# Longer instructions in the body and a halved row at the end of a ReLU row-sum on one Trainium2 core

## The chip, the cores and the metric

The kernel runs on one core of a Trainium2 chip. The metric is the device time of one execution in microseconds (us), without the host. The profile of an execution covers a *span* that begins with the kernel's first DMA issue and ends with its last wait. The time is longer than the span, by 1.35 us in the kernel before (called *time outside the span* below). A result lists the time and the span of every run; spans are listed to 0.1 us.

Engine names in the profile: DVE is VectorE, ACT is ScalarE, SPq is the sequencer that issues the DMAs. A *semaphore* is a counter: in the kernel's code one engine or a DMA raises it (`then_inc`), and another engine waits until it has reached a value (`wait_ge`).

## The reference

```python
x = np.random.randn(32, 512, 1024).astype(np.float32)
out = np.sum(np.maximum(x, 0), axis=-1)          # (32, 512) float32
```

64 MiB are read and 64 KiB are written.

## The kernel before

The 16,384 rows lie on 128 partitions, 128 rows per partition. Seven chunks of 16 rows per partition (8 MiB each) come first. Then comes the tail: transfers of 8, 4, 2 and 1 rows (the one-row transfer is *row 14*), then the last row in three parts of 576, 256 and 192 columns. Three chunk buffers rotate. The tail reuses the buffer of chunk 4, so it can be issued only when VectorE has finished that chunk.

```python
STEPS = [4, 5, 7]; MIXED = [3, 4, 5]
TAIL = [8, 4, 2, 1]; LAST = [576, 256, 192]
# issue on the SP queue: chunk c waits until VectorE has done chunk c - 3
for c in range(NBIG + 1):
    if c >= NB:
        sp.wait_ge(s_dve, 3 * (c - NB + 1))
    if c < NBIG:
        sp.dma_start(out=buf[:, c % NB, :, :], in_=...).then_inc(s_in[c], 16)
# ... the tail's transfers, then (later) the two stores

# chunks 0 to 5: ScalarE does the ReLU in place, VectorE sums the rows
for i, n in enumerate(steps):
    t = buf[:, b, r : r + n, :]
    act.activation(t, t, AF.Relu).then_inc(s_act, 1)
    dve.wait_ge(s_act, 3 * c + i + 1)
    dve.tensor_reduce(out=res[...], in_=t, axis=X, op=ALU.add).then_inc(s_dve, 1)
# ... chunk 6 and the tail: whole rows, ReLU and sum in one instruction, alternating engines

# the last row
act.wait_ge(s_in[-3], 16)
on_act(parts[0], last[:, n : n + 1]).then_inc(s_tact, 1)
dve.wait_ge(s_in[-2], 16)
on_dve(parts[1], last[:, n + 1 : n + 2]).then_inc(s_tpart, 1)
dve.wait_ge(s_tpart, 1)
dve.wait_ge(s_in[-1], 16)
dve.wait_ge(s_tact, 1)
on_dve(last[:, :], res[:, J - 1 : J]).then_inc(s_tdve, 1)   # third part plus the two partial sums
```

## Time and profile before

| | before |
|---|---|
| time, median of 3 runs | 161.24 us (161.21 to 161.25) |
| span of the profiled run (161.23 us) | 159.88 us |
| time outside the span, that run | 1.35 us |
| VectorE busy / ScalarE busy | 122.0 / 101.0 us |
| input DMA | 434 GB/s while it streams |

These are lines of the profile page: the span, each engine's busy time (share of the span, number of instructions), the DMA queues (packets, MB, share of the 16 engines' time), and the chain of waits by line.

```profile
span 159.9 us, 148 instructions
...
DVE 122.0 (76%) x58; ACT 101.0 (63%) x55; POOL 0.2 (0%) x4
...
q1 hardware_dynamic: 2304, 67.18, 97.9%
q14 instruction: 1, 0.01, 0.0%
...
DMA buf<-in_x_dram 69%; ACT buf L129 18%; DVE res L131 10%; DVE buf L112 1%; SPq L89 1%; DVE last L112 0%; DVEq L163 0%
```

The data queue (q1) occupies the DMA engines for 97.9% of the span. Queue q14, which the page lists as instruction, carried one packet of 8 KiB (0.01 MB on the page); it comes up again below.

Next is the table by stages of the kernel before. Each line is a stretch between the arrivals of two chunks: its bounds, its length, busy time and count for VectorE, ScalarE and GpSimd, then granted clock, DMA share and GB/s.

```profile
core 0: us, DVE busy (x) ACT busy (x) POOL busy (x), PEclk, DMA share, GB/s
21.84:41.19 19.35, 15.12 (x3) 14.04 (x4) 0.00 (x0) 1.00 1.00 434
...
99.23:118.59 19.36, 17.48 (x4) 14.04 (x4) 0.00 (x0) 1.00 1.00 433
118.59:137.94 19.35, 17.59 (x9) 12.71 (x8) 0.00 (x0) 1.00 0.94 406
```

An 8 MiB chunk arrives every 19.35 us, at 434 GB/s, and no engine needs that long for it (VectorE at most 17.59 us, ScalarE 14.04), so the body is bound by input DMA. (The 0.94 in the last stretch does not mean a gap: the arrivals keep their period.)

Finally, the timeline of the kernel before: start, duration, engine, source line, operation, operands, count, and in brackets the idle time before and what ended it.

```profile
21.84 14.04 ACT L129 ACTIVATE buf<-buf 128x4096 f32<-128x4096 f32 x3 [19.77 <-DMA buf<-in_x_dram]
25.48 9.85 DVE L131 TENSOR_REDUCE res<-buf 128x4 f32<-128x4096 f32 x2 [25.48 <-ACT buf L129]
...
120.95 1.82 SPq L89 DMA_DIRECT2D buf<-in_x_dram  x4
...
156.32 1.22 DVE L112 TENSOR_SCALAR_CACHE_REDUCE buf<-buf 128x1024 f32<-128x1024 f32 x1
157.08 0.68 ACT L109 ACTIVATE buf<-buf 128x576 f32<-128x576 f32 x1 [0.90 <-DMA buf<-in_x_dram]
157.47 0.08 DVE L112 DVE_READ_ACCUMULATOR buf<-buf 128x1 f32 x1
157.47 0.41 DVE L112 TENSOR_SCALAR_CACHE_REDUCE buf<-buf 128x256 f32<-128x256 f32 x1
...
158.02 0.36 DVE L112 TENSOR_SCALAR_CACHE_REDUCE last<-last 128x194 f32<-128x194 f32 x1
...
158.41 0.34 SPq L168 DMA_DIRECT2D out_dram<-res  x1
```

Row 14 lands at 156.30. VectorE then works through row 14, the 256 columns, three waits and the last part one after the other. The last 192 columns landed at 157.68 (the DMA completions in the trace), yet the last instruction starts only at 158.02: at the end VectorE, not DMA, holds the kernel for about 0.34 us.

### The profile page before, as it was taken

Reading aid. Unit: us, or ns where it says so; the run is one execution under the profiler, and the core shown is the slowest. Engines: PE = TensorE matmul, PEld = TensorE weight load, DVE = VectorE, ACT = ScalarE, POOL = GpSimd, SP = SyncE. Lnnn points to the kernel's source line nnn. Section 1 sums busy time; section 2 is a strip of 40 time slices with the busy share of each in tenths; the row PEclk is TensorE's granted clock in tenths of the full one; section 3 lists DMA queues with packets and bytes.
Section 4 is the critical chain, followed back from the end, with each engine's and each line's share of the span. In section 5 each row is a group of like instructions: output and inputs, shape, how many; then the busy total and the mean of one; then the engine's idle time right before and its main releaser. Section 6 shows DMA issues by size and latency. Waiting matters only on the chain.

```text
span 159.9 us, 148 instructions
## 1 busy us (share of the span) xinstructions
DVE 122.0 (76%) x58; ACT 101.0 (63%) x55; POOL 0.2 (0%) x4
## 2 busy tenths in 40 slices
DVE  0000006989879897998969989699899999598995
ACT  3000059990699808996099941999339980496972
POOL 0000000000000000000000000000000000000000
DMA  7996996996996997989979969969969969899993
GB/s 262 525 525 262 525 525 262 525 525 262 525 492 295 525 459 328 525 377 410 525 312 476 525 262 525 525 262 525 525 262 525 525 262 525 385 402 394 414 407 116
DMA packets 2305, 67.18 MB, mean 420 GB/s; under 512 B 512, under 2 KB 768, under 8 KB 1024
## 3 DMA queue, kind: packets, MB, share of 16 engines
q1 hardware_dynamic: 2304, 67.18, 97.9%
q14 instruction: 1, 0.01, 0.0%
HBM read 67.11 MB, written 0.07 MB: 420 GB/s over the span
## 4 chain that ended last, share of the span: by engine, by line
DMA 69%; ACT 18%; DVE 11%; SPq 1%; issue 0%; DVEq 0%
DMA buf<-in_x_dram 69%; ACT buf L129 18%; DVE res L131 10%; DVE buf L112 1%; SPq L89 1%; DVE last L112 0%; DVEq L163 0%
## 5 line engine op out<-in xcount | busy, mean ns | idle before, releaser
L131 DVE TENSOR_REDUCE res<-buf 128x4 f32<-128x4096 f32 (+3 forms) x18 | 100.4, 5604 | 33.6 <-ACT buf L129 33.6
L129 ACT ACTIVATE buf<-buf 128x4096 f32<-128x4096 f32 (+3 forms) x18 | 80.8, 4553 | 46.3 <-DMA buf<-in_x_dram 46.3
L109 ACT ACTIVATE buf<-buf 128x1024 f32<-128x1024 f32 (+1 forms) x18 | 18.4, 1024 | 9.8 <-DMA buf<-in_x_dram 9.8
L112 DVE TENSOR_SCALAR_CACHE_REDUCE buf<-buf 128x1024 f32<-128x1024 f32 (+1 forms) x19 | 21.3, 1173 | 2.7 <-DMA buf<-in_x_dram 2.5
L109 ACT ACTIVATION_READ_ACCUMULATOR buf<-buf 128x1 f32 x18 | 3.4, 186 | 0.0
L129 ACT ACT_TABLE_LOAD x1 | 1.3, 1283 | 0.8 <-PEq L184 0.8
L112 DVE DVE_READ_ACCUMULATOR buf<-buf 128x1 f32 x19 | 1.6, 83 | 0.0
L112 DVE TENSOR_SCALAR_CACHE_REDUCE last<-last 128x194 f32<-128x194 f32 x1 | 0.4, 356 | 0.1
L184 POOL MEMSET const-bfloat16-1.0<- 128x1 bf16 x1 | 0.1, 102 | 0.0
L184 POOL MEMSET const-uint8-127<- 128x1 uint8 x1 | 0.1, 102 | 0.0
L184 POOL MEMSET const-float32-0.0<- 128x1 f32 x1 | 0.1, 100 | 0.2 <-issue 0.2
L184 POOL MEMSET const-float32-1.0<- 128x1 f32 x1 | 0.1, 99 | 0.0
L112 DVE DVE_READ_ACCUMULATOR last<-last 128x1 f32 x1 | 0.1, 83 | 0.0
## 6 DMA issues: line engine op xcount, KB each, us to landing
buf<-in_x_dram SPq DMA_DIRECT2D x1, 4096.0 KB, 26.7
buf<-in_x_dram SPq DMA_DIRECT2D x1, 2048.0 KB, 31.2
buf<-in_x_dram SPq DMA_DIRECT2D x1, 1024.0 KB, 33.2
buf<-in_x_dram SPq DMA_DIRECT2D x1, 512.0 KB, 34.0
buf<-in_x_dram SPq DMA_DIRECT2D x1, 288.0 KB, 34.3
buf<-in_x_dram SPq DMA_DIRECT2D x1, 128.0 KB, 34.1
buf<-in_x_dram SPq DMA_DIRECT2D x7, 36.3
last<-in_x_dram SPq DMA_DIRECT2D x1, 96.0 KB, 33.9
```

The lines of the kernel that those rows point to most:

```text
L89: sp.dma_start(out=buf[:, tb, r : r + n, :], in_=xv[-1][:, r : r + n, :]).then_inc(s_in[NBIG + i], 16)
L109: return act.activation(t, t, AF.Relu, accum_out=acc)
L112: return dve.tensor_scalar(out=t, in0=t, scalar1=0.0, scalar2=None, op0=ALU.max, op1=ALU.add, accum_out=acc)
L129: act.activation(t, t, AF.Relu).then_inc(s_act, 1)
L131: dve.tensor_reduce(out=res[:, c * BIG + r : c * BIG + r + n], in_=t, axis=X, op=ALU.add).then_inc(s_dve, 1)
L184: nc = _bacc.Bacc("TRN2", target_bir_lowering=False, num_devices=1)
```

## The change

The intent has two parts. In the body, fewer instructions with less fixed cost (estimated from the groups by form of the kernel before, about 0.15 us for each reduce on VectorE and 0.2 us for each activation on ScalarE): chunk 0 in one step of 16 rows, chunks 1 to 3 in steps of 7 and 9. At the end, a shorter serial chain on VectorE: row 14 is split between the two engines, and the last row is cut 512, 256, 256. The diff, cut to its core:

```diff
-STEPS = [4, 5, 7]
-MIXED = [3, 4, 5]
+STEPS = [[16], [7, 9], [7, 9], [7, 9], [4, 5, 7], [3, 4, 5]]
-LAST = [576, 256, 192]
+LAST = [512, 256, 256]
+    half = nc.alloc_sbuf_tensor("half", [P, 2], fp32)
...
-            sp.wait_ge(s_dve, 3 * (c - NB + 1))
+            sp.wait_ge(s_dve, done[c - NB])
...
+    r, _, s = tail[-1]
+    act.wait_ge(s, 16)
+    dve.wait_ge(s, 16)
+    on_act(buf[:, tb, r, 0 : D // 2], half[:, 0:1]).then_inc(s_half, 1)
+    on_dve(buf[:, tb, r, D // 2 : D], half[:, 1:2]).then_inc(s_half, 1)
+    dve.wait_ge(s_half, 2)
+    dve.tensor_tensor(
+        out=res[:, j0 + r : j0 + r + 1], in0=half[:, 0:1], in1=half[:, 1:2], op=ALU.add
+    )
...
-    dve.wait_ge(s_tpart, 1)
+    dve.wait_ge(s_part, 2)
     dve.wait_ge(s_in[-1], 16)
-    dve.wait_ge(s_tact, 1)
```

More of the change, by code (lines that the diff above doesn't have):

```diff
@@ L6 @@
 BIG = 16
-NTWO = 6
 NB = 3
@@ L57, in bass_relu_sum_kernel @@
     s_fdve = nc.alloc_semaphore("s_fdve")
-    s_tact = nc.alloc_semaphore("s_tact")
-    s_tpart = nc.alloc_semaphore("s_tpart")
+    s_half = nc.alloc_semaphore("s_half")
+    s_part = nc.alloc_semaphore("s_part")
     s_tdve = nc.alloc_semaphore("s_tdve")
@@ L64, in bass_relu_sum_kernel @@
     sp, act, dve = nc.sync, nc.scalar, nc.vector
+    NTWO = len(STEPS)
+    done = [sum(map(len, STEPS[: c + 1])) for c in range(NTWO)]
     tb = NBIG % NB
@@ L117, in row @@
         return buf[:, c % NB, i, :], res[:, c * BIG + i : c * BIG + i + 1]
-    for c in range(NTWO):
-        b, steps = c % NB, STEPS if c < NTWO - 1 else MIXED
+    k = 0
+    for c, steps in enumerate(STEPS):
         act.wait_ge(s_in[c], 16)
-        if steps is MIXED:
+        alone = BIG - sum(steps)
+        if alone:
             dve.wait_ge(s_in[c], 16)
-            for i in (BIG - 4, BIG - 3):
+            for i in range(BIG - alone, BIG - alone // 2):
                 on_dve(*row(c, i))
         r = 0
-        for i, n in enumerate(steps):
-            t = buf[:, b, r : r + n, :]
+        for n in steps:
+            t = buf[:, c % NB, r : r + n, :]
             act.activation(t, t, AF.Relu).then_inc(s_act, 1)
-            dve.wait_ge(s_act, 3 * c + i + 1)
+            k += 1
+            dve.wait_ge(s_act, k)
             dve.tensor_reduce(
@@ L134, in bass_relu_sum_kernel @@
             r += n
-        if steps is MIXED:
-            for i in (BIG - 2, BIG - 1):
-                on_act(*row(c, i))
+        for i in range(BIG - alone // 2, BIG):
+            on_act(*row(c, i))
     j0 = NBIG * BIG
@@ L147, in bass_relu_sum_kernel @@
                 ins.then_inc(s_fact if i % 2 else s_fdve, 1)
-    for r, n, s in tail:
-        if n > 1:
-            act.wait_ge(s, 16)
+    for r, n, s in tail[:-1]:
+        act.wait_ge(s, 16)
         dve.wait_ge(s, 16)
@@ L154, in bass_relu_sum_kernel @@
             f(buf[:, tb, i, :], res[:, j0 + i : j0 + i + 1])
+    r, _, s = tail[-1]
+    act.wait_ge(s, 16)
+    dve.wait_ge(s, 16)
[5 more added lines that the diff above has]
+    )
     n = LAST[2]
     act.wait_ge(s_in[-3], 16)
-    on_act(parts[0], last[:, n : n + 1]).then_inc(s_tact, 1)
+    on_act(parts[0], last[:, n : n + 1]).then_inc(s_part, 1)
     dve.wait_ge(s_in[-2], 16)
-    on_dve(parts[1], last[:, n + 1 : n + 2]).then_inc(s_tpart, 1)
-    dve.wait_ge(s_tpart, 1)
+    on_dve(parts[1], last[:, n + 1 : n + 2]).then_inc(s_part, 1)
+    dve.wait_ge(s_part, 2)
     dve.wait_ge(s_in[-1], 16)
-    dve.wait_ge(s_tact, 1)
     on_dve(last[:, :], res[:, J - 1 : J]).then_inc(s_tdve, 1)
```

## The prediction

> **What bounds the kernel now.** Input DMA, from end to end. The table by stages shows 434 GB/s and DMA share 1.00 in every stretch between chunk arrivals, and the timeline shows ACT starting on a new 8 MiB chunk at 21.84, 41.19, 60.54, 79.88, 99.23, 118.59 and 137.94 us: a period of 19.35 us, with no gap. [...] VectorE is busy 122.0 of 159.9 us (page, part 1). Only two places can move the time: a chunk's DMA issued too late, and the 3.6 us after the one-row transfer lands at 156.30.
>
> **Body: fewer, longer instructions.** From the groups by form, tensor_reduce takes 4418/5486/7620 ns for 4/5/7 rows, so 1.042 ns per element plus 0.15 us each; ScalarE 3614/4452/6160 ns, so 0.83 ns plus about 0.2. Estimates: 16 rows take 17.2 us on VectorE and 13.85 on ScalarE; 9 rows 9.75 and 7.85. The 18 pairs become 13, five pairs fewer, under 0.5 us of VectorE work saved, none of it critical. What is added is latency: in chunk 0, VectorE now starts at about 35.7 instead of 25.5 and ends at about 53 instead of 43.5. From there VectorE hardly idles:
> - chunk 3 issued at about 53 (chunk 2 lands 60.5)
> - chunk 4 at 70.2 (79.9)
> - chunk 5 at 87.5 (99.2)
> - chunk 6 at 104.8 (118.6)
> - tail transfers from 122.2 (before: 120.95), needed by 137.9
>
> The thinnest margin is 7.5 us, so the queue does not run dry and the 19.35 us period stays. VectorE ends chunk 5 at about 137.6 (before: 136.2), 0.3 us before chunk 6 lands; the 0.50 us idle before 147.64 absorbs an error. Body: 0 us.
>
> **End.** Now: row 14 on VectorE 156.32 to 157.5, then the 256 columns to 157.89, then three waits, then the last instruction at 158.02 to 158.39 (timeline, chain of waits). The last 192 columns had already landed at 157.68 (DMA completions), so VectorE, not DMA, held the last 0.34 us. After: each engine takes half of row 14. Estimates: VectorE to 157.0, ScalarE with accumulator read to 157.05[...]. 512 columns land at 157.0, 256 at 157.35, the last 256 at 157.7. ScalarE's 512: 157.05 to 157.8. VectorE's 256: 157.37 to 157.8. Then the last instruction waits for both, starts at about 157.9, and is 64 elements longer (0.42 against 0.36): ends about 158.3. The DMA arrival of the second part and the larger last part take most of the freed time back. Gain 0.05 to 0.1 us.
>
> **Predicted time.** 161.24 - 0.07, so 161.17 us; 8-in-10 range 160.95 to 161.40. Faster by over 2%: 0.01; within 2%: 0.98; slower by over 2%: 0.01.
>
> **What would show it.** ACT's chunk starts unchanged to 0.05 us; VectorE's first reduce about 17.2 us from about 35.7, then idle below 1 us until 137.5; input DMA still about 434 GB/s; the last VectorE instruction starting at 157.85 to 157.95, released by the other 256-column part or ScalarE rather than following row 14.
>
> **What would make it wrong.** A queue that needs its next transfer more than 7 us ahead; an add or wait chain on row 14 longer than 0.35 us, which delays the 256 columns; VectorE arriving more than 1 us late at chunk 6.

The forecast's sum came to 161.24 - 0.07 = 161.17 us. The add entered it only through the assumption that it would be done before the 256 columns landed (157.35), so that it would not delay them.

## The result, and the profile after

| | before | after |
|---|---|---|
| time, median of 6 runs | 161.24 us (161.20 to 161.25) | 161.37 us (161.26 to 161.91) |
| mean of the 6 runs | 161.23 us | 161.50 us |
| ratio of the fast runs | 1 | 1.0017 (95% interval 1.0000 to 1.0034) |
| span of the profiled run | 159.88 us | 159.69 us |
| time outside the span, profiled run | 1.35 us | 1.58 us |

Ratios are the mean time of one kernel's fast runs over that of the other's of the same rounds, so they are not quite the ratio of the medians. All runs here count as fast: none is 1.5% above the fastest of its kernel.

The profile shows a span 0.19 us *shorter*, and the time is *longer*. Every one of the six changed runs was slower than every one of the six before. Two of them, at 161.84 and 161.91 us, with spans of 159.7 and 160.0, stand out with 1.9 to 2.1 us outside the span.

The page of the changed kernel, the same parts as before:

```profile
span 159.7 us, 141 instructions
...
DVE 120.4 (75%) x54; ACT 101.2 (63%) x52; POOL 0.2 (0%) x4
...
q1 hardware_dynamic: 2304, 67.18, 98.0%
...
DVE res L135 54%; DMA buf<-in_x_dram 34%; ACT buf L132 9%; SPq L91 1%; SPq L99 0%; DVE buf L114 0%; DVE last L114 0%
```

There are seven instructions fewer, ScalarE has 52 in place of 55, and no instruction packet falls in the span. The last line invites a false reading: VectorE's reduces now make up 54% of the chain. The table by stages of the changed kernel says otherwise:

```profile
core 0: us, DVE busy (x) ACT busy (x) POOL busy (x), PEclk, DMA share, GB/s
21.75:41.10 19.35, 5.46 (x1) 13.86 (x1) 0.00 (x0) 1.00 1.00 434
...
99.14:118.50 19.36, 19.36 (x4) 14.04 (x3) 0.00 (x0) 1.00 1.00 433
118.50:137.84 19.34, 18.42 (x8) 12.71 (x7) 0.00 (x0) 1.00 0.94 407
```

The arrivals keep their 19.35 us. VectorE is now busy for whole stretches because it works on a backlog, but the backlog still ends in time (0.92 us before chunk 6, in the timeline below). The chain of the changed kernel in order of time (start, length, what) shows why it names VectorE nevertheless:

```profile
35.64 86.04 DVE res L135 x10
...
123.99 33.28 DMA buf<-in_x_dram
```

The chain goes from a landing back to the *issue* of that transfer and from there to VectorE, which freed the buffer. But the transfer took 33.28 us from issue to landing, nearly all of it queued behind earlier transfers (it is 128 KiB, which at the measured 434 GB/s is 0.3 us by estimate). So an issue a little earlier or later changes nothing: the tail was issued 0.74 us later than before (next view), and row 14 landed no later. A chain that contains such a long DMA step is not a statement about what limits the kernel.

The timeline of the changed kernel:

```profile
21.75 13.86 ACT L132 ACTIVATE buf<-buf 128x16384 f32<-128x16384 f32 x1 [19.68 <-DMA buf<-in_x_dram]
35.64 86.03 DVE L135 TENSOR_REDUCE res<-buf 128x16 f32<-128x16384 f32 x10 [35.64 <-ACT buf L132]
...
121.69 1.77 SPq L91 DMA_DIRECT2D buf<-in_x_dram  x4
...
137.84 1.22 DVE L114 TENSOR_SCALAR_CACHE_REDUCE buf<-buf 128x1024 f32<-128x1024 f32 x1 [0.92 <-DMA buf<-in_x_dram]
...
156.24 0.63 ACT L111 ACTIVATE buf<-buf 128x512 f32<-128x512 f32 x1
156.24 0.69 DVE L114 TENSOR_SCALAR_CACHE_REDUCE buf<-buf 128x512 f32<-128x512 f32 x1
...
156.94 0.63 ACT L111 ACTIVATE buf<-buf 128x512 f32<-128x512 f32 x1
156.99 0.16 DVE L164 TENSOR_TENSOR res<-half 128x1 f32<-128x1 f32 x1
157.29 0.42 DVE L114 TENSOR_SCALAR_CACHE_REDUCE buf<-buf 128x256 f32<-128x256 f32 x1
...
157.76 0.42 DVE L114 TENSOR_SCALAR_CACHE_REDUCE last<-last 128x258 f32<-128x258 f32 x1
...
158.21 0.34 SPq L179 DMA_DIRECT2D out_dram<-res  x1
```

VectorE starts at 35.64, the tail is issued 0.74 us later than before (121.69 against 120.95), and VectorE is still idle for 0.92 us before chunk 6. At the end, row 14 lands at 156.22. From its landing to the issue of the final store the changed kernel takes 1.99 us (158.21 - 156.22), the kernel before 2.11 us (158.41 - 156.30). So 0.12 us of the 0.19 us is the new ending; the remaining 0.08 us is there already when the first chunk lands (21.73 against 21.81). The second is within chance: the first activation, which follows that landing by 0.02 to 0.03 us, starts at 21.84 us before and 21.75 after, and in later profiles at 21.75 (e9), 21.80 (e5) and 21.87 us (e6); the spans of the kernel before lie between 159.7 and 160.1 us in its nine runs beside e5 to e8.

### The profile page after: what moved, and what is told of

Read it like the earlier page. It is cut to its first block, busy times and chain, and to the rows that moved or that the text cites. A ratio compares the mean times of both kernels' runs of the same rounds, so it can differ in the third digit from the quotient of the medians.

```text
span 159.7 us, 141 instructions
## 1 busy us (share of the span) xinstructions
DVE 120.4 (75%) x54; ACT 101.2 (63%) x52; POOL 0.2 (0%) x4
## 4 chain that ended last, share of the span: by engine, by line
DVE 54%; DMA 34%; ACT 9%; SPq 1%; issue 0%
DVE res L135 54%; DMA buf<-in_x_dram 34%; ACT buf L132 9%; SPq L91 1%; SPq L99 0%; DVE buf L114 0%; DVE last L114 0%
## 5 line engine op out<-in xcount | busy, mean ns | idle before, releaser
L135 DVE TENSOR_REDUCE res<-buf 128x7 f32<-128x7168 f32 (+5 forms) x13 | 99.1, 7692 | 35.6 <-ACT buf L132 35.6
L132 ACT ACTIVATE buf<-buf 128x7168 f32<-128x7168 f32 (+5 forms) x13 | 80.4, 6233 | 46.7 <-DMA buf<-in_x_dram 46.7
L111 ACT ACTIVATE buf<-buf 128x1024 f32<-128x1024 f32 (+1 forms) x19 | 19.0, 1000 | 9.0 <-DMA buf<-in_x_dram 8.9
L114 DVE TENSOR_SCALAR_CACHE_REDUCE buf<-buf 128x1024 f32<-128x1024 f32 (+2 forms) x19 | 20.9, 1146 | 2.0 <-DMA buf<-in_x_dram 1.7
```

What stands on the lines that cost most here:

```text
L111: return act.activation(t, t, AF.Relu, accum_out=acc)
L114: return dve.tensor_scalar(out=t, in0=t, scalar1=0.0, scalar2=None, op0=ALU.max, op1=ALU.add, accum_out=acc)
L135: dve.tensor_reduce(out=res[:, c * BIG + r : c * BIG + r + n], in_=t, axis=X, op=ALU.add).then_inc(s_dve, 1)
```

## The experiments

Each kernel was timed in five runs beside nine of the kernel before on the same chip, in sessions of four kernels: e1 to e4, e5 to e8, e9 to e12, e13 to e16. Each session ran on another chip; the kernel before had 1.36 to 1.37 us outside the span in each, so the sessions can be compared. All outputs were correct. "Outside" is the mean over the runs of time minus span, good to about 0.03 us because spans are listed to 0.1. The program lengths are instructions counted in the built program, waits that stand alone included; an instruction with an accumulator counts twice, as the profile shows it (before: 20 TENSOR_SCALAR_CACHE_REDUCE and 20 DVE_READ_ACCUMULATOR on VectorE, 18 ACTIVATION_READ_ACCUMULATOR on ScalarE). The length of ScalarE's program is the profile's ScalarE count plus those waits (55 + 2 = 57 before).

| run | ScalarE, VectorE length | median us | before, same session | mean span | outside |
|---|---|---|---|---|---|
| before (36 runs) | 57, 61 | | 161.26 to 161.29 | 159.91 | 1.37 |
| after (first result) | 54, 57 | 161.37 | 161.24 | 159.78 | 1.72 |
| e1 after again | 54, 57 | 161.40 | 161.29 | 159.84 | 1.57 |
| e2 body only | 52, 56 | 161.72 | 161.29 | 159.92 | 1.78 |
| e3 tail only | 59, 62 | 161.33 | 161.29 | 159.76 | 1.57 |
| e4 halves, old parts | 54, 57 | 161.39 | 161.29 | 159.86 | 1.55 |
| e5 after, padded | 57, 61 | 161.09 | 161.27 | 159.76 | 1.35 |
| e6 before, longer | 59, 62 | 161.38 | 161.27 | 159.90 | 1.50 |
| e7 body only, padded | 57, 61 | 161.24 | 161.27 | 159.88 | 1.35 |
| e8 after, VectorE padded | 54, 61 | 161.25 | 161.27 | 159.74 | 1.54 |
| e9 after, ScalarE padded | 57, 57 | 161.20 | 161.26 | 159.80 | 1.37 |
| e10 after, padded less | 56, 60 | 161.46 | 161.26 | 159.88 | 1.55 |
| e11 body only, padded some | 54, 57 | 161.65 | 161.26 | 159.98 | 1.66 |
| e12 after, padded, again | 57, 61 | 161.15 | 161.26 | 159.82 | 1.36 |
| e13 before, ScalarE +1 | 58, 61 | 161.31 | 161.29 | 159.90 | 1.40 |
| e14 before, VectorE +1 | 57, 62 | 161.25 | 161.29 | 159.92 | 1.35 |
| e15 after, ScalarE +2 | 56, 57 | 161.29 | 161.29 | 159.82 | 1.51 |
| e16 after, ScalarE +4 | 58, 57 | 161.26 | 161.29 | 159.82 | 1.48 |

### First: is it real, and which part brings it?

**e1** is the changed kernel without any edit.

> The changed kernel, unchanged, for a larger sample. Theory 1 (the extra time lies outside the span that the profile shows, and comes with this program): the profiled span is again about 0.2 us shorter than that of the kernel before (159.7 against 159.9), yet the fastest runs stay at 161.26 or above, and about a third of the runs fall at 161.4 to 161.9. Theory 2 (the excursions were chance, of one session on the chip): all runs agree within 0.1 us, at 161.05 to 161.3.

The runs lay between 161.31 and 161.49, ratio 1.0010 (0.9997 to 1.0022). No run went beyond 161.49, so the excursions of the first result did not come back here. But the time outside the span stayed at 1.57 us against 1.37, so theory 2 falls for that part: the extra 0.2 us outside comes with the program. The span was shorter by 0.06 us on average, not 0.2.

**e2** changes the body alone; the old tail is kept:

```diff
 STEPS = [[16], [7, 9], [7, 9], [7, 9], [4, 5, 7], [3, 4, 5]]
-LAST = [512, 256, 256]
+LAST = [576, 256, 192]     # and the tail's code as in the kernel before
```

> Only the longer instructions of the first four transfers; the old last rows (row 14 whole, 576, 256, 192). Theory 1a (the longer instructions bring the extra time and the excursions): runs between 161.3 and 161.9, the spread of the changed kernel. Theory 1b (the new last rows bring them): a tight group at 161.15 to 161.3, the span equal to that of the kernel before within 0.1 us, because the chunk period stays 19.35 us.

Measured: 161.59 to 161.77, ratio 1.0027 (1.0013 to 1.0040), with a mean span (159.92) equal to that of before (159.90) and 1.78 us outside. This is the slowest variant, and nothing of it shows in the span.

**e3** changes the tail alone:

```diff
-STEPS = [[16], [7, 9], [7, 9], [7, 9], [4, 5, 7], [3, 4, 5]]
+STEPS = [[4, 5, 7]] * 5 + [[3, 4, 5]]
```

> Only the new last rows (row 14 halved, 512, 256, 256); the old 4, 5, 7 rows in the body. Theory 1a: a tight group about 0.1 us below the kernel before (161.05 to 161.2), since the last instruction should end 0.1 us earlier. Theory 1b: the spread of the changed kernel, 161.26 to 161.9.

The span fell by 0.14 us (159.76 against 159.90), the share expected of the tail. But the time did not fall: 161.33, with 1.57 us outside. So neither 1a nor 1b holds. *Both* halves of the change raise the time outside the span, one with shorter programs (e2) and one with longer ones (e3). That suggested a property of the programs rather than of the work.

**e4** keeps the halved row and goes back to the old cut of the last row:

```diff
-LAST = [512, 256, 256]
+LAST = [576, 256, 192]
```

> The changed kernel with the last row cut 576, 256, 192 again, so row 14 is still halved. My account of the end: the last landing and the last instruction's release stay within 0.1 us, the last VectorE instruction is 64 elements shorter (0.36 against 0.42 us), ScalarE's part 64 elements longer, so the span is within 0.05 us of the changed kernel's. If the 512 cut were what costs the time, the runs would fall back to a tight group at 161.1 to 161.25.

Span 159.86 against 159.84 in e1, time 161.39 against 161.40: the cut of the last row costs and gains nothing that can be seen.

### Second: program length against the work itself

Theory P: the time outside the span depends on the length of the engines' programs. Rival W: the changed work brings it. The padding is waits for a semaphore that has long reached its value, placed where the engine idles (in e5 the 35.79 us before VectorE's first reduce and 5.56 us before ScalarE's chunk 1); two waits make one instruction (e5's fourteen raise the page's count from 141 to 148). **e5** is the changed kernel, padded back to the lengths of before:

```diff
     k = 0
+    for _ in range(8):
+        dve.wait_ge(s_in[0], 16)
     for c, steps in enumerate(STEPS):
+        for _ in range(6 if c == 1 else 0):
+            act.wait_ge(s_in[0], 16)
         act.wait_ge(s_in[c], 16)
```

> The changed kernel with waits that are already satisfied added to ScalarE (six, three instructions) and VectorE (eight, four instructions), placed where both engines idle, so that each engine's program is as long as in the kernel before. Theory P (the time outside the span depends on the length of the engines' programs): the profiled span stays at 159.7 to 159.9, the part outside it falls from 1.57 to 1.72 us to about 1.37 us, and the time to about 161.15 to 161.25. Rival W (the extra time belongs to the work that was changed: the halved row, the long instructions): it stays at 161.4, with 1.57 us or more outside.

Measured: 161.03 to 161.22, 1.35 us outside. Seven instructions that do nothing made the changed kernel 0.3 us faster than its unpadded runs.

**e6** adds four such waits to ScalarE (two instructions) and two to VectorE (one) in the kernel before.

```diff
+    for _ in range(2):
+        dve.wait_ge(s_in[0], 16)
     for c in range(NTWO):
         b, steps = c % NB, STEPS if c < NTWO - 1 else MIXED
+        for _ in range(4 if c == 1 else 0):
+            act.wait_ge(s_in[0], 16)
         act.wait_ge(s_in[c], 16)
```

> The kernel before with the same satisfied waits, two instructions more on ScalarE and one more on VectorE, so as long as the kernel that changed the last rows alone (which had 1.57 us outside the span). Theory P: about 1.57 us outside the span instead of 1.37, so 161.4 to 161.5 us with an unchanged span of 159.9. Rival W: the same as the kernel before, 161.25 to 161.3.

Measured: 161.38, 1.50 us outside (1.40 to 1.61 in single runs), span unchanged. The kernel before, with no change to its work, takes on extra time, 0.13 us of the 0.2 us that e3 showed at the same lengths. That e3 reached these lengths without padding also speaks against the waits themselves as the cause.

**e7** is e2 with ten waits (five instructions) on each engine, in the places of e5:

```diff
+    for _ in range(10):                        # VectorE
+        for _ in range(10 if c == 1 else 0):   # ScalarE
```

> Only the longer instructions of the first four transfers, with five satisfied-wait instructions added to each of ScalarE and VectorE so that both programs are again as long as before. Theory P: 1.37 us outside the span and 161.25 to 161.3 us in all, where without the padding it had 1.78 us and 161.70. Rival W (the long instructions bring it): 161.6 to 161.75 again.

Measured: 161.24, 1.35 us outside, where e2 had 161.72 and 1.78. The longer instructions of the body cost nothing once the length is restored. Rival W falls.

### Third: which engine, and how wide is the good range?

From here on only the two counts of waits differ, in the same places:

```diff
-VectorE range(8), ScalarE range(6)      # e5 and e12, the changed kernel
+VectorE range(8), ScalarE none          # e8, the changed kernel
+VectorE none,     ScalarE range(6)      # e9, the changed kernel
+VectorE range(6), ScalarE range(4)      # e10, the changed kernel
+VectorE range(2), ScalarE range(4)      # e11, the body alone (e2)
+VectorE none,     ScalarE range(2)      # e13, the kernel before
+VectorE range(2), ScalarE none          # e14, the kernel before
+VectorE none,     ScalarE range(4)      # e15, the changed kernel
+VectorE none,     ScalarE range(8)      # e16, the changed kernel
```

**e8** has the eight VectorE waits of e5 alone.

> The changed kernel with the padding on VectorE alone (four instructions); ScalarE is three shorter than before. If VectorE's program length alone sets the time outside the span: 1.37 us outside, about 161.2. If ScalarE's does: 1.57 us or more, 161.4. Rival W: 161.4 too.

**e9** has the six ScalarE waits of e5 alone.

> The changed kernel with the padding on ScalarE alone (three instructions, so as long as before); VectorE is four shorter. Theory P, both engines matter: between the padded (1.35 us outside the span) and the unpadded (1.57 to 1.72), so 1.4 to 1.6 us, as with VectorE alone padded (1.54). If ScalarE's length alone decides: 1.35 us, 161.1. Rival W, the work itself: 1.57 us or more.

e8 stayed at 1.54 us outside, e9 fell to 1.37. So the three instructions on ScalarE carry the effect.

**e10** has four ScalarE waits and six VectorE waits (one instruction less on each than e5).

> The changed kernel padded by one instruction less on each of ScalarE and VectorE than the one that fell to 161.1. Theory P with a window of several instructions: 1.35 us again. With a window of one instruction: about 1.55 us outside the span and 161.3.

Measured: 1.55 us outside. One instruction less on each engine loses it.

**e11** is e2 with four ScalarE waits and two VectorE waits, as long as the changed kernel.

> Only the longer instructions in the body, padded by two instructions on ScalarE and one on VectorE, so that both programs are as long as in the changed kernel, not as in the kernel before. Theory P: as much time outside the span as the changed kernel has, 1.57 to 1.72 us, in place of 1.78 (no padding) and 1.35 (full padding); with its span of 159.9, 161.45 to 161.6 us. If any padding at all helped: 1.35 us.

Measured: 1.66 us outside, 161.65. So it is not "any padding at all helps". One run of the five was at 162.04, with 2.14 outside, as in the first result; the other four had 1.47 to 1.59.

**e12** repeats e5.

> The changed kernel with the full padding once more, to see whether it beats both kernels: about 161.1 us, 0.1 to 0.2 us below the kernel before of the same rounds, with 1.35 us outside the span and a span 0.1 us shorter.

Measured: 161.15 against 161.26 of before in the same session, ratio 0.9993 (0.9981 to 1.0006); e5 had 0.9990 (0.9977 to 1.0004). Each interval includes 1. The span was shorter by 0.10 us on average (159.82 against 159.92), the time outside the same. The two runs agree on about 0.1 us, but that is all they can say.

The last four runs separate the two engines by one instruction each. **e13** is the kernel before with two more ScalarE waits, **e14** with two more VectorE waits, **e15** and **e16** the changed kernel with four and eight more ScalarE waits.

> The kernel before with one satisfied-wait instruction more on ScalarE (58), VectorE unchanged. If ScalarE's length decides and 57 is the only good value: 1.5 us or more outside the span and 161.4. If 57 to 58 is good: 1.36 us and 161.27. If VectorE's length decided: 1.36 us.

> The kernel before with one satisfied-wait instruction more on VectorE, ScalarE unchanged at 57. If ScalarE's length alone decides: 1.36 us outside the span, 161.27. If VectorE's counts as well: 1.5 us or more, 161.4.

> The changed kernel with two instructions more on ScalarE (56), VectorE as changed (57). If ScalarE's length decides, as with 56 and 60 earlier: about 1.55 us outside the span, 161.4.

> The changed kernel with four instructions more on ScalarE (58), VectorE as changed (57). Must agree with e13 if ScalarE's length alone decides: both 1.36 us outside the span (161.15), or both 1.5 us or more (161.4).

With VectorE fixed at 57 the sweep over ScalarE's length gives 1.57 (54, e1), 1.51 (56, e15), 1.37 (57, e9) and 1.48 (58, e16). Four runs of e16 lay between 1.36 and 1.43 and the fifth was an excursion at 161.66 us, 1.86 outside; e13, also at 58, had 1.40. With ScalarE fixed at 57, VectorE at 57, 61 and 62 gives 1.37, 1.35 and 1.35. So ScalarE's length decides; VectorE's does not within what was tried at 57. (VectorE at 60 was tried only with 56 on ScalarE, in e10: 1.55, against 1.51 in e15.) 57 is the best of the values tried, 58 nearly as good in its typical run, and 56 and 59 are worse. Over all 61 runs with 57 instructions (the 36 of before among them) the time outside stayed between 1.31 and 1.41 us. Values of 1.8 us and above came only at other lengths.

### What stays open

Why ScalarE's length matters is not settled. The first guess was the packets that the page lists as instruction on queue q14. The queue seems to bear it out at first: one such packet in the span of before and of e5, none in that of the changed kernel. Header and queue lines of e5:

```profile
span 159.7 us, 148 instructions
...
q1 hardware_dynamic: 2304, 67.18, 97.9%
q14 instruction: 1, 0.01, 0.0%
```

But e9 is as good as e5 (1.37) and has no such packet:

```profile
span 159.7 us, 144 instructions
...
q1 hardware_dynamic: 2304, 67.18, 98.0%
```

And e6, which is slow, has one:

```profile
q1 hardware_dynamic: 2304, 67.18, 98.0%
q14 instruction: 1, 0.01, 0.0%
```

So the packet is no marker of the slow case. The trace does not say which engine it belongs to, but in the seven pages at hand it goes with VectorE's length: q14 is listed where VectorE has 61 or 62 instructions (one packet in before, e5 and e6, two in e14) and not where it has 56 or 57 (e2, the changed kernel and e9). In the kernel before the packet starts 0.19 us before the span's end (read from the packed trace).

The packed traces of before and after also record semaphore updates after the span (no view of the profile prints them). The last one comes 1.46 us after the span's end in before and 1.47 us in after, while the time outside the span is 1.35 and 1.58 us. So the last recorded update does not come later by the extra 0.23 us. Where the measured time begins and ends is not recorded either: the last update of before lies later than its 1.35 us of time outside. Neither the pages nor these two traces show what causes the extra time.

## Why the prediction was right or wrong

The prediction gave 161.17 us with a range of 160.95 to 161.40. The median was 161.37, at the edge, and the mean of the fast runs was 161.50, outside. The sign was wrong too.

- **Right: the body costs and gains nothing.** The chunk period stayed 19.35 us; the span of the body alone (e2) was 159.92 against 159.90. VectorE's 16-row reduce took 17.22 us (predicted 17.2), ScalarE's activation 13.86 us (predicted 13.85). VectorE ended chunk 5 at 136.9, earlier than the predicted 137.6, and idled 0.92 us, so the margin was larger than feared. (One term was too small: the prediction saved under 0.5 us of VectorE work, and e2 saved 1.3 us, 120.7 against 122.0 busy. It is not critical.)
- **Right: the ending gains about a tenth.** Predicted 0.05 to 0.1 us; from row 14's landing to the store's issue it gained 0.12 us, and the tail alone (e3) shortened the span by 0.14 us. The one-element add took 160 ns and ended at 157.15, 0.14 us before VectorE began the 256 columns (157.29), so it did not delay them, as the sum assumed. The last instruction began 1.54 us after row 14's landing (157.76 - 156.22), where 157.9 - 156.3 = 1.6 was predicted.
- **Wrong: the step "161.24 - 0.07".** It carried the difference between time and span, 1.35 us before, into the sum as a constant. It is not one: it measured 1.57 us (e1) to 1.72 us (first result) in the changed kernel. The change removed three instructions from ScalarE's program, and this, not the work, added 0.20 us in e1, where the span gained 0.06, and 0.35 us in the first result, two excursions included, where it gained about 0.1. With three instructions of padding on ScalarE (e9), or seven on both engines (e5, e12), the kernel ran at 161.20, 161.09 and 161.15 us, 0.06 to 0.18 us below before of the same sessions, as the prediction's sum would have it, though each of these ratios has an interval that includes 1. Why the length of ScalarE's program matters stays open.
- **Wrong as well: what was listed as able to go wrong.** A dry queue, a slow add and a late VectorE were named; all three lie inside the span. The excursions to 161.8 and 161.9 us also come from outside it.

## What to carry to other kernels

When a change promises a tenth of a microsecond, compare time *and* span: if the span falls and the time does not, the loss lies outside the span, and no reading of the timeline will find it. Test then with padding that does nothing, on one engine at a time, before blaming an instruction: here one instruction less on ScalarE cost 0.14 us of time outside the span (e15 against e9), more than the 0.12 us that the rearranged ending had gained in the profile. And a chain of waits that runs through a DMA with 33 us from issue to landing says who issued it, not what limits the kernel; the period of the arrivals says that.
